# Ten slots for small statistics in place of six, and weight halves that start 128 bytes later in every partition

## The chip, the cores and the metric

The kernel runs on one core of a Trainium2 chip. The metric is the time of one execution on the device, in microseconds; the kernel before takes 1837.65 us, the median of 3 runs. A profiled execution of its own gives the rows shown here: it has the start and the length of each instruction on each engine.

## The reference, cut to what matters

The reference is three transformer layers for 256 tokens of width 1024, in float32. The first block has a retention layer and a differential-attention layer, each with a gated feed-forward net (hidden width 2816); its first layer also carries 256 context tokens. The second block is a token mixer with two attentions and a recurrence, and a squared-ReLU net of hidden width 4096. Nearly all arithmetic is products of a 256-row activation with large weight matrices:

```python
ux = modulate(rms_norm(h_x, norm_g[l, 0]), shm, scm)
p = u @ w_in                                                   # 1024 x 8192, 3072, 6728
val, gate = jnp.split(u @ w_up, 2, axis=-1)
return (jax.nn.silu(dwconv3(gate, conv_w, conv_b)) * val) @ w_down
...
def rms_norm(x, g):
    x32 = x.astype(jnp.float32)
    y = x32 * lax.rsqrt(jnp.mean(x32 * x32, axis=-1, keepdims=True) + EPS)
```

## The kernel before, in words

**Weights in halves.** Weights come from memory one MB at a time into a tile `st` (128 partitions of 2048 floats, two slots). `split_w` cuts each `st` into two tiles `hl`, each of 128 partitions of 2 x 1024 floats (8192 bytes in a partition): part 0 is a rounded copy in the type fp32r, written by ScalarE (L120), and part 1 is the rest that the rounding left, written by VectorE (L121). Tag `hl` has five slots. In a few places the halves go to a slot of tag `big` instead ("wide" halves). Activations are split in the same way into an upper and a lower tile, and these lie in `big` slots always (14 slots of 8192 bytes).

**Three products for one.** With both operands split, each product is three matmuls into one PSUM sum: upper by upper, upper by lower, lower by upper. There are two forms.

- Form A (`mm3`, L129 to L131): the stationary operand is 128 columns of a weight half (`hl`), the moving operand is 256 columns of an activation (`big`). The profile writes it `ps<-big,hl 128x256`.
- Form B (`rows_mm3`, L408 to L410): the stationary operand is 128 columns of an activation (`big`), the moving operand is 512 columns of a weight half (`hl`), written `ps<-hl,big 128x512` or `at<-hl,big 128x512`. The retention product uses form B with both operands in `big` (`at<-big,big`), and so do products with wide halves. `form_b` uses it with 256 columns for the first tiles of the last two up-projections (`ps<-hl,big 128x256`, and `ps<-big,big 128x256` where the halves are wide).

Before each matmul its stationary operand is loaded (row `PEld`); that load runs while the matmul before it still streams its moving operand.

**Small statistics.** `tiny` gives tiles of 1 to 8 floats in a partition, of which each slot takes 32 bytes. `rms2` (L147, L150) and `retain` (L773, L775) write a sum of squares into one, a sum with the epsilon into the next, and `power` (L140, on GpSimd) its inverse square root into a third; `shift_bias` and `top_keys` take some as well. A tag hands its slots out in turn; an instruction that writes a slot waits for what still uses it.

**Where the tags lie.** The pool `sp` lays its tags one behind another in each partition, in the order in which they are first asked for. As the program is built (bytes in a partition, read from its list of allocations):

| tag | slots x bytes | first byte before | first byte after |
|---|---|---|---|
| `mid` | 4 x 4096 | 20,416 | 20,416 |
| `big` | 14 x 8192 | 36,800 | 36,800 |
| `tiny` | 6 (10) x 32 | 151,488 | 151,488 |
| `junk` | 1 x 2048 | 151,680 | 151,808 |
| `sml` | 4 x 2048 | 153,728 | 153,856 |
| `st` | 2 x 8192 | 161,920 | 162,048 |
| `hl` | 5 x 8192 | 178,304 | 178,432 |
| `s1`, `ph_b`, `ph_a` | 5 x 1024, 2 x 2048 | 219,264 | 219,392 |

All operands of both forms start at a multiple of 512 bytes behind the start of their slot. So each start in `big` is 448 beyond a multiple of 512, each start in `hl` 128 beyond one before the change and 256 after it. The text calls "distance" the start of the moving operand less that of the stationary one, counted modulo 512:

| operands | distance before | after |
|---|---|---|
| form A: moving `big`, stationary `hl` | 320 | 192 |
| form B and `form_b`: moving `hl`, stationary `big` | 192 | 320 |
| both in `big` | 0 | 0 |

Of the kernel before, what the change touches and what calls it, by code (L numbers as in the profile page):

```python
# [32 lines left out]
def block_kernel(ctx: ExitStack, tc: tile.TileContext, A, out):  # L33
# [4 lines left out]
    sp = ctx.enter_context(tc.tile_pool(name="sp", bufs=2))  # L38
# [5 lines left out]
    def nm(base):  # L44
        n_name[0] += 1
        return f"{base}_{n_name[0]}"
# [13 lines left out]
        return sp.tile(shape, dt, tag="sml", bufs=4, name=nm("sml"))  # L60

    def tiny(shape, dt=F32):
        return sp.tile(shape, dt, tag="tiny", bufs=6, name=nm("tiny"))

    def junk():
        return sp.tile([P, 512], F32, tag="junk", bufs=1, name=nm("junk"))
# [71 lines left out]
    def power(v, width=1):  # L138
        r = tiny([P, width])
        G.tensor_tensor(r, v, nhalf[:, 0:width], op=ALU.pow)  # L140
        return r

    def rms2(halves, n):

        ss = tiny([P, 2])
        for i in range(2):
            S.activation(junk()[:, 0:halves[i].shape[-1]], halves[i], AF.Square, scale=n ** -0.5,  # L147
                         accum_out=ss[:, i:i + 1])
        v = tiny([P, 1])
        V.tensor_scalar(v, ss[:, 0:1], ss[:, 1:2], EPS, op0=ALU.add, op1=ALU.add)  # L150
        return power(v)
# [1435 lines left out]
```

## Time and profile before

| | |
|---|---|
| median of 3 runs | 1837.65 us (1836.05 to 1839.79) |
| the profiled execution | 1835.11 us |
| its span, first to last instruction | 1833.3 us |
| TensorE busy with matmuls | 1804.6 us, 98% |
| VectorE, ScalarE, GpSimd busy | 1242.5, 897.2, 176.4 us |
| granted TensorE clock | 1.000 |
| DMA queue 1, share of the 16 engines | 52.0% |

The length of a matmul in the profile runs to the end of its results, and it overlaps the next one. What a matmul costs is the distance from its start to the start of the next. The text calls that its pace. A view of a window gives it: of a window in which TensorE never stops, the window and the length of one matmul together (it also counts the ones cut by its edges), divided by the count behind the x. From a timeline it is the start of the last row less that of the first, divided by the rows between.

### The profile page before, as it was taken

What the parts mean: (1) busy time and instruction counts of PE and PEld (TensorE: products, weight loads), DVE (VectorE), ACT (ScalarE), POOL (GpSimd) and SP (SyncE); (2) the same over time, 40 slices, a digit from 0 to 9 for tenths busy, and PEclk for the clock granted to TensorE, in tenths of its full rate; (3) what the DMA queues carried; (4) which work ended last, traced back from release to release, by engine and by line L of the source; (5) the groups of instructions that cost most, each with busy time, mean ns of one, the idle gap of its engine ahead of it and who ended that gap; (6) DMA issues with size and microseconds to landing.
All of it is one profiled execution on the core that took longest, in us unless ns stands there. A gap on an engine that the chain in (4) does not pass through costs nothing.

```text
span 1833.3 us, 28048 instructions
## 1 busy us (share of the span) xinstructions
PE 1804.6 (98%) x11300; PEld 1566.1 (85%) x11300; DVE 1242.5 (68%) x1921; ACT 897.2 (49%) x1460; POOL 176.4 (10%) x178
## 2 busy tenths in 40 slices
PE   9999999999999999999999989999999999999998
PEld 8878787797778999899988766799879999989986
DVE  5874674957567977487847676877664787566644
ACT  6542342323355644364536555754454575455633
POOL 0212212032100000000000020100010001120000
PEclk9999999999999999999999999999999999999999
DMA  8553543738668555555554422455646524545553
GB/s 317 180 193 132 194 151 106 238 127 267 211 235 291 202 185 188 188 174 187 192 201 151 176 93 93 133 176 179 215 155 231 180 93 161 170 161 189 190 188 115
DMA packets 59849, 330.34 MB, mean 180 GB/s; under 512 B 7207, under 2 KB 10424, under 8 KB 27720
## 3 DMA queue, kind: packets, MB, share of 16 engines
q1 hardware_dynamic: 59432, 328.47, 52.0%
q8 instruction: 88, 1.44, 0.3%
q14 instruction: 41, 0.34, 0.1%
q10 hardware_dynamic: 288, 0.09, 0.0%
HBM read 323.75 MB, written 4.79 MB: 179 GB/s over the span
## 4 chain that ended last, share of the span: by engine, by line
PE 85%; DVE 5%; DMA 3%; issue 2%; ACT 2%; POOL 1%; SPq 0%; POOLq 0%; ACTq 0%; DVEq 0%
PE ps L129 10%; PE ps L130 10%; PE ps L131 10%; PE at L408 7%; PE at L410 7%; PE at L409 7%; PE ps L408 6%; PE ps L409 6%; PE ps L410 6%; PE nr L130 2%; PE nr L131 2%; PE nr L129 2%; DVE hl L121 1%; PE at L129 1%; PE at L131 1%
## 5 line engine op out<-in xcount | busy, mean ns | idle before, releaser
L121 DVE TENSOR_TENSOR hl<-st,hl 128x1024 fp32r<-128x1024 f32 x460 | 564.0, 1232 | 343.7 <-ACT hl L120 341.6
L120 ACT ACTIVATE hl<-st 128x1024 fp32r<-128x1024 f32 x462 | 484.9, 1056 | 382.4 <-PE at L410 140.2
L129 PE MATMUL ps<-big,hl 128*128 128x256 f32 x1540 | 433.6, 282 | 1.2 <-DVE s L1324 1.0
L131 PE MATMUL ps<-big,hl 128*128 128x256 f32 x1540 | 430.7, 280 | 0.0
L130 PE MATMUL ps<-big,hl 128*128 128x256 f32 x1540 | 430.5, 280 | 0.0
L129 PEld LDWEIGHTS ps<-big,hl 128*128 128x128 f32 x1540 | 289.4, 188 | 5.7 <-issue 2.3
L130 PEld LDWEIGHTS ps<-big,hl 128*128 128x128 f32 x1540 | 289.6, 188 | 0.4 <-issue 0.2
L131 PEld LDWEIGHTS ps<-big,hl 128*128 128x128 f32 x1540 | 289.2, 188 | 0.1
L408 PE MATMUL ps<-hl,big 128*128 128x512 f32 (+1 forms) x588 | 230.9, 393 | 0.5 <-ACT big L962 0.3
L410 PE MATMUL ps<-hl,big 128*128 128x512 f32 (+1 forms) x588 | 227.5, 387 | 0.9 <-DVE big L316 0.9
L409 PE MATMUL ps<-hl,big 128*128 128x512 f32 (+1 forms) x588 | 227.4, 387 | 0.0
L410 PE MATMUL at<-hl,big 128*128 128x512 f32 x532 | 211.1, 397 | 0.0
L408 PE MATMUL at<-hl,big 128*128 128x512 f32 x532 | 210.7, 398 | 0.2 <-DVE sml L332 0.2
L409 PE MATMUL at<-hl,big 128*128 128x512 f32 x532 | 210.9, 397 | 0.0
L198 DVE SCALAR_TENSOR_TENSOR big<-mid,cs,big 128x1024 f32<-128x1024 f32 x112 | 143.7, 1325 | 11.1 <-DMA mid<-in_ada_w_dram 10.8
L408 PEld LDWEIGHTS ps<-hl,big 128*128 128x128 f32 x588 | 110.7, 188 | 36.5 <-issue 8.1
L410 PEld LDWEIGHTS ps<-hl,big 128*128 128x128 f32 x588 | 110.7, 188 | 25.3 <-DVE big L316 1.3
L409 PEld LDWEIGHTS ps<-hl,big 128*128 128x128 f32 x588 | 110.8, 188 | 23.8 <-DVE hl L121 0.8
L410 PEld LDWEIGHTS at<-hl,big 128*128 128x128 f32 x532 | 100.1, 188 | 24.2 <-issue 0.8
L408 PEld LDWEIGHTS at<-hl,big 128*128 128x128 f32 x532 | 100.0, 188 | 24.2 <-DVE sml L332 0.7
L140 POOL TENSOR_TENSOR tiny<-tiny,nhalf 128x1 f32<-128x1 f32 (+1 forms) x48 | 35.6, 742 | 876.7 <-DVE tiny L150 698.5
L409 PEld LDWEIGHTS at<-hl,big 128*128 128x128 f32 x532 | 100.1, 188 | 23.0
(298 smaller groups left out, 2581.4 us busy)
## 6 DMA issues: line engine op xcount, KB each, us to landing
st<-in_ffn_up_dram SPq DMA_DIRECT2D x66, 1024.0 KB
mid<-in_ada_w_dram SPq DMA_DIRECT2D x80, 512.0 KB
st<-in_ffn_down_dram SPq DMA_DIRECT2D x33, 1024.0 KB
st<-in_mix_in_dram SPq DMA_DIRECT2D x31, 1024.0 KB
st<-in_ret_in_dram SPq DMA_DIRECT2D x28, 1024.0 KB
st<-in_diff_in_dram SPq DMA_DIRECT2D x20, 1024.0 KB
st<-in_ret_out_dram SPq DMA_DIRECT2D x16, 1024.0 KB
st<-in_mlp_up_dram SPq DMA_DIRECT2D x16, 1024.0 KB
```

Of the source, the lines that this page charges most:

```text
L120: S.activation(hl[:, 0, :], src, AF.Copy)
L121: (G if wide // 2 else V).tensor_tensor(hl[:, 1, :], src, f32(hl[:, 0, :]), op=ALU.subtract)
L129: T.matmul(o, lh, rh, start=start, stop=False)
L130: T.matmul(o, lh, rl, start=False, stop=False)
L131: T.matmul(o, ll, rh, start=False, stop=stop)
L140: G.tensor_tensor(r, v, nhalf[:, 0:width], op=ALU.pow)
L198: V.scalar_tensor_tensor(acc[:, s, :], t, cs[:, k, s:s + 1], acc[:, s, :], op0=ALU.mult, op1=ALU.add)
L408: T.matmul(o, xh, wh, start=start, stop=False)
L409: T.matmul(o, xh, wl, start=False, stop=False)
L410: T.matmul(o, xl, wh, start=False, stop=stop)
```

## The change

Tag `tiny` gets ten slots in place of six. Four slots of 32 bytes are 128 bytes, and the tags behind `tiny` lie that much further on. `big` and `mid` stay where they were.

```diff
     def tiny(shape, dt=F32):
-        return sp.tile(shape, dt, tag="tiny", bufs=6, name=nm("tiny"))
+        return sp.tile(shape, dt, tag="tiny", bufs=10, name=nm("tiny"))
```

No instruction is added, taken away or moved on any engine. What differs in the order are waits. On ScalarE, in the four retention products of the second head (`retain`), the piece of the difference reads as follows (each L773 writes the sums of one product, each L120 is an upper weight half of the next product):

```order
 L773 ACTIVATE junk_1326,tiny_1312<-at_1314 128x512 [waits PE_49,Activation_49]
-L773 ACTIVATE junk_1348,tiny_1336<-at_1337 128x512 [waits DVE_49,PE_49,Activation_49]
+L773 ACTIVATE junk_1348,tiny_1336<-at_1337 128x512 [waits PE_49,Activation_49]
 L773 ACTIVATE junk_1362,tiny_1336<-ps_1338 128x512 [waits PE_49,Activation_49]
-L773 ACTIVATE junk_1387,tiny_1372<-at_1373 128x512 [waits DVE_49,PE_49,Activation_49]
+L773 ACTIVATE junk_1387,tiny_1372<-at_1373 128x512 [waits PE_49,Activation_49]
 L773 ACTIVATE junk_1398,tiny_1372<-at_1374 128x512 [waits PE_49,Activation_49]
 L693 ACTIVATE big_1408<-ps_1417 128x256 [waits PE_49,Pool_49]
-L120 ACTIVATE hl_1659<-st_1654 128x1024 [waits PE_49]
+L120 ACTIVATE hl_1659<-st_1654 128x1024 [waits DVE_49,PE_49]
```

The wait of the sums for VectorE, which read the slot two products earlier, goes; the weight halves behind it now name VectorE themselves.

## Rows read from the trace of the kernel before

**Rows 1.** The page: busy time, DMA queue, and the chain that ended last
```profile
PE 1804.6 (98%) x11300; PEld 1566.1 (85%) x11300; DVE 1242.5 (68%) x1921; ACT 897.2 (49%) x1460; POOL 176.4 (10%) x178
...
q1 hardware_dynamic: 59432, 328.47, 52.0%
...
PE 85%; DVE 5%; DMA 3%; issue 2%; ACT 2%; POOL 1%; SPq 0%; POOLq 0%; ACTq 0%; DVEq 0%
PE ps L129 10%; PE ps L130 10%; PE ps L131 10%; PE at L408 7%; PE at L410 7%; PE at L409 7%; PE ps L408 6%; PE ps L409 6%; PE ps L410 6%; PE nr L130 2%; PE nr L131 2%; PE nr L129 2%; DVE hl L121 1%; PE at L129 1%; PE at L131 1%
```

**Rows 2.** Groups by line and shape: xcount | busy us, mean ns | idle before
```profile
L121 DVE TENSOR_TENSOR hl<-st,hl 128x1024 fp32r<-128x1024 f32 x460 | 564.0, 1232 | 343.7 <-ACT hl L120 341.6
L129 PE MATMUL ps<-big,hl 128*128 128x256 f32 x1540 | 433.6, 282 | 1.2 <-DVE s L1324 1.0 <-ACT s L1107 0.2
...
L408 PE MATMUL ps<-hl,big 128*128 128x512 f32 x540 | 217.3, 402 | 0.3 <-ACT big L962 0.3
...
L408 PE MATMUL at<-hl,big 128*128 128x512 f32 x532 | 210.7, 398 | 0.2 <-DVE sml L332 0.2
...
L129 PE MATMUL nr<-big,hl 128*128 128x256 f32 x240 | 67.1, 280 | 0.0
L129 PE MATMUL at<-big,hl 128*128 128x256 f32 x220 | 62.7, 285 | 1.5 <-DVE s L1324 1.5
...
L408 PE MATMUL at<-big,big 128*128 128x512 f32 x108 | 42.7, 400 | 0.6 <-DVE big L778 0.6
...
L408 PE MATMUL ps<-hl,big 128*128 128x256 f32 x48 | 13.6, 283 | 0.2
```

**Rows 3.** Windows of form A (distance 320), TensorE alone: busy (count), clock, DMA
```profile
core 0: us, PE busy (x), PEclk, DMA share, GB/s
620.00:720.00 100.00, 100.00 (x851) 1.00 0.55 186
...
1212.00:1300.00 88.00, 88.00 (x750) 1.00 0.55 186
1681.00:1736.00 55.00, 55.00 (x469) 1.00 0.57 189
```

**Rows 4.** The same view: the first, the longest and the last of seven other windows
```profile
1192.00:1198.00 6.00, 6.00 (x55) 1.00 0.47 188
1402.00:1427.00 25.00, 25.00 (x223) 1.00 0.62 216
...
1662.00:1667.50 5.50, 5.50 (x51) 1.00 0.34 140
```

**Rows 5.** Timeline of two runs with 256 columns moving from `hl`, first and last
```profile
1184.65 0.28 PE L408 MATMUL ps<-hl,big 128*128 128x256 f32 x1
...
1186.89 0.28 PE L409 MATMUL ps<-hl,big 128*128 128x256 f32 x1
...
1653.03 0.28 PE L410 MATMUL ps<-hl,big 128*128 128x256 f32 x1
...
1656.09 0.28 PE L410 MATMUL ps<-hl,big 128*128 128x256 f32 x1
```

**Rows 6.** Timeline of a run with 256 columns, both operands in `big`, first and last
```profile
1187.48 0.28 PE L408 MATMUL ps<-big,big 128*128 128x256 f32 x1
...
1190.96 0.28 PE L410 MATMUL ps<-big,big 128*128 128x256 f32 x1
```

**Rows 7.** 512 columns: a window from `hl`; first and last of a run from `big`
```profile
1740.00:1820.00 80.00, 80.00 (x345) 1.00 0.49 168
...
250.48 0.39 PE L408 MATMUL at<-big,big 128*128 128x512 f32 x1
...
261.81 0.39 PE L410 MATMUL at<-big,big 128*128 128x512 f32 x1
```

**Rows 8.** What ended the idle time before line L773: us, times
```profile
  PE at L410: 8.5, 7
  issue: 7.3, 4
```

## The prediction

> **What bounds the kernel now.** I read the page first. TensorE is busy for 98% of the span and stands for 85% of the chain that ended last; VectorE, the next, is busy for 68% [rows 1]. In the groups by line, almost no idle time stands before the matmuls of form A and form B: 1.2 us before 1540 of them, 0.3 us before 540 [rows 2]. So the time is a sum of paces of matmuls. The granted clock is 1.00 (the 2.4 GHz level) in all windows used below [rows 3, 4, 7], so no difference of pace among them comes from the clock.
>
> Then I read paces from windows in which TensorE never stops. Form A runs at (100 + 0.28) / 851 = 117.8 ns, and again at 117.7 and 117.9 ns in windows far apart [rows 3]. But in seven other windows, with 491 counted matmuls, the same form with operands in the same tags runs at 113.4 ns (25.28 / 223) or close to it [rows 4]. So form A has a narrow and a wide pace, 4.4 ns apart. A long window of either holds it to its end: what a stretch begins with, it keeps. The address alone does not decide it, since nothing differs between those windows in the starts modulo 512.
>
> The place of the operands does matter. With 256 columns and both operands in `big` (distance 0) the pace is 3.48 us over 29 steps, 120.0 ns [rows 6]. With the moving operand in `hl` (distance 192) one run has 3.06 us over 27 steps, 113.3 ns, and another 2.24 us over 19 steps, 117.9 ns [rows 5]: the two paces of form A again. With 512 columns from `hl` the pace is 80.39 / 345 = 233.0 ns, and with both in `big` 11.33 us over 50 steps, 226.6 ns [rows 7]. Shape, type and clock are the same in each pair, and only the tag of an operand differs. The next stationary operand is loaded while the moving one streams, both out of the same partitions; a likely reading is that the two reads get in each other's way more or less by where they lie. That reading is mine; the paces are the trace's.
>
> **The change part by part.** It changes two things.
>
> First, waits. The statistics in `tiny` no longer wait for a slot's reader of two products ago. What ended ScalarE's idle time before L773 is the matmul whose result it squares, or "issue", 7.3 us in 4 places; no reader of a slot stands there [rows 8]. The order of all engines is the same. I take 0, with bounds of 0 and 7.3 us gained, if all of that "issue" were the slot and all lay on the path. A loss is excluded: a wait taken out cannot come later, and the waits that now name VectorE before L120 ask for work that the old wait ahead of it on ScalarE had already covered.
>
> Second, addresses. `st` moves by 128 bytes too, as a target of DMA; the queue's packets take 52.0% of the engines' time [rows 1], so twice nothing is lost there even if each packet took some per cent longer or shorter: 0. ScalarE and VectorE read and write `st` and `hl`; an L121 takes 1232 ns and stands 343.7 us idle in all [rows 2], so some per cent either way there is hidden under the matmuls: 0.
>
> What is left is the matmuls. Form A has three times 1540 + 240 + 220, that is 6000 of them; form B from `hl` has three times 540 + 532, that is 3216 [rows 2]. The change swaps their distances: form A goes from 320 to 192, form B from 192 to 320. Products with both operands in `big` keep theirs.
>
> *Form A.* The only rows that show 256 columns at distance 192 are those of `form_b` (48 a line [rows 2]). Both paces occur there. I count its stretches in the timeline as mostly narrow; the wide one of [rows 5] follows a pause. In form A now, the seven narrow windows hold 491 of 6000, so about 5500 are wide. Bounds: all narrow, 5500 x 4.4 = 24 us gained; all at the pace of distance 0, 5500 x 2.2 + 500 x 6.6 = 15 us lost. I take four fifths of the 5500 narrow: 5500 x 0.8 x 4.4 = 19.4 us gained, because distance 192 is the nearest row. Form A's lines have about 38% of the chain [rows 1], 697 us, against 6000 x 117.4 = 704 us of pace: nearly all of it counts.
>
> *Form B.* No row shows 512 columns at distance 320. The nearest are 226.6 ns at distance 0 and 233.0 ns at 192. Bounds: the step of 6.4 ns down, 3216 x 6.4 = 21 us gained, and the same step up, 21 us lost. There is no reason in the rows for either, and the pace from `hl` is one value in the long stretches; I take 0.
>
> The sum: 1835.1 us of the profiled execution, less 19.4, is 1815.7. The median of the runs shown is 2.5 us above that execution, so I expect 1818 us.
>
> A rule of the Trainium skill speaks against any effect. "TensorE: Matmul & The Clock Gate", part 2, says that TensorE has two independent read ports into SBUF, and that loading the next weights takes no bandwidth from the matmul that runs; it gives a pace of N / 2.4 + 2.5 ns, 109 ns for 256 columns and 216 ns for 512. By that rule the change is worth 0. The trace does not agree: 113.4, 117.8 and 120.0 ns for one shape, 226.6 and 233.0 ns for the other [rows 3 to 7].
>
> **The rivals.**
>
> *Nothing changes.* The distances 320 and 192 differ by 128 and both leave 64 modulo 128, while distance 0 leaves 0. If only that remainder counts, all paces stay. For it: the two paces of form A and of `form_b` are equal, 117.8 and 113.4 against 117.9 and 113.3 ns [rows 3 to 5]. Against it: how seldom form A is narrow now. It gives 1837.7 us, and less the bound of the waits 1830. The skill's rule of two ports ends here too.
>
> *Form B slows by a step.* Slower: 3216 x 6.4 = 21 us, if form A stays as it is; 1858 us. The place is each product with weights moving, above all the last stretch, 80 us at 233.0 ns without a pause [rows 7]. It decides as soon as the pace of form B rises more than 6 ns, for then 19.4 us of form A no longer pay for it. For it: between distance 0 and 192 the two shapes went opposite ways (120.0 to 113.3 ns with 256 columns, 226.6 to 233.0 with 512), so a swap that helps the one may hurt the other. Against: by that same pattern form B would go down if form A's old 117.8 ns is what distance 320 means.
>
> *Both gain.* Form B falls to the 226.6 ns of distance 0 and form A becomes narrow: 1818 less 21, 1797 us.
>
> **How the numbers follow.** A measurement of this kernel tells about 0.2%, 3.7 us, from no change. Chances: one of the two forms gains about 20 us, 0.36 (mostly form A, my forecast); both gain, 0.08; the waits alone gain more than 3.7 us, 0.01. Faster: 0.45. Nothing changes, or form A's gain is eaten by form B: 0.27. Form B slower with form A as it is, 0.16, form A slower toward 120.0 ns, 0.09, both slower, 0.03: slower, 0.28. The range, 1796 to 1858 us, reaches from both gaining to form B's step up and leaves out some 1 in 10. Where only form A's share of narrow stretches is uncertain, from a third of the 24 us gained to all of it, the range of the forecast itself is 1813 to 1830 us.
>
> **What would show it.** In the profile after, the windows of long form A stretches, now near 117.8 ns, should stand at 113.4 ns, and the last stretch of form B at 233 ns still. The mean length of L129 should fall below 282 ns. TensorE's idle time, the lengths of L120 and L121 and the DMA share should not move. I am wrong if the pace of form A stays at 117.8 ns, or if form B's last stretch leaves 233 ns by more than 2 ns; which of the two moved, and by how much, then gives the time: 6 us for each nanosecond of form A, 3.2 us for each of form B.

## The result, and the profile after

The changed kernel takes 1806.08 us, the median of 4 runs (1804.03 to 1808.72); beside it, the kernel before takes 1836.85 us (also 4 runs). The ratio is 0.9836, with a 95% interval of 0.9824 to 0.9849; the medians lie 30.8 us apart. The forecast was 1818 us in a range of 1796 to 1858, faster with a chance of 0.45. The profiled execution takes 1804.03 us, with a span of 1802.2 us, 31.1 us below that of before, at a mean granted clock of 0.999.

The page of the changed kernel, with the lines that answer to [rows 1]:

```profile
PE 1776.8 (99%) x11300; PEld 1547.9 (86%) x11300; DVE 1242.6 (69%) x1921; ACT 896.4 (50%) x1460; POOL 173.3 (10%) x178
...
q1 hardware_dynamic: 59432, 328.47, 52.7%
...
PE 88%; DVE 5%; issue 2%; ACT 2%; DMA 1%; POOL 1%; SPq 0%; POOLq 0%; DVEq 0%; ACTq 0%
```

TensorE's busy time fell by 27.8 us with the same 11300 matmuls, its idle time from 28.7 to 25.4 us. VectorE, ScalarE and the packets of the queue did what they did before: 52.7% of 1802.2 us is 950 us, 52.0% of 1833.3 us was 953. So nearly all of the time came out of the matmuls themselves. The groups by line and shape, as in [rows 2]:

```profile
L121 DVE TENSOR_TENSOR hl<-st,hl 128x1024 fp32r<-128x1024 f32 x460 | 565.9, 1237 | 316.8 <-ACT hl L120 314.1
...
L129 PE MATMUL ps<-big,hl 128*128 128x256 f32 x1540 | 430.2, 279 | 0.8 <-DVE s L1324 0.7
...
L408 PE MATMUL ps<-hl,big 128*128 128x512 f32 x540 | 216.6, 401 | 0.3 <-ACT big L962 0.3
...
L408 PE MATMUL at<-hl,big 128*128 128x512 f32 x532 | 207.6, 392 | 0.3 <-DVE sml L332 0.3
```

L129 fell from 282 to 279 ns, and L408 with `at` from 398 to 392. These are lengths that overlap; what a matmul costs is its pace, and the windows give that. Windows of TensorE alone, the first three in form A and the last in form B (they answer to [rows 3] and [rows 7]; the same stretches come some 8 to 31 us earlier now):

```profile
core 0: us, PE busy (x), PEclk, DMA share, GB/s
612.00:708.00 96.00, 96.00 (x849) 1.00 0.55 190
...
1192.00:1276.00 84.00, 84.00 (x743) 1.00 0.56 191
1655.00:1706.00 51.00, 51.00 (x452) 1.00 0.56 195
...
1709.00:1794.00 85.00, 85.00 (x373) 1.00 0.48 161
```

Form A: 96.28 / 849 = 113.4 ns, and again 84.28 / 743 = 113.4 and 51.28 / 452 = 113.5, where 117.8 stood. Form B: 85.39 / 373 = 228.9 ns, where 233.0 stood. Both forms became faster at the same clock. Not all of form A did. The next windows of the same kernel show two pairs, each a stretch of form A with a stretch of form B right behind it:

```profile
148.00:169.00 21.00, 21.00 (x180) 1.00 0.25 87
171.00:186.00 15.00, 15.00 (x66) 1.00 0.46 142
711.00:769.00 58.00, 58.00 (x255) 1.00 0.59 203
```

In the first of them form A, at 148 us, is wide, 21.28 / 180 = 118.2 ns, and form B behind it has 15.39 / 66 = 233.2 ns. The form A stretch at 612 us is narrow, and form B behind it, at 711 us, has 58.39 / 255 = 229.0. The experiments come back to this.

Since the trace has the start of each matmul, all steps from one start to the next can be added up by form:

| steps, added up, in us | before | after | |
|---|---|---|---|
| form A, 6000 | 715.6 | 695.5 | -20.1 |
| form B from `hl`, 3215 | 761.2 | 750.8 | -10.4 |
| the other products of both forms | 160.1 | 160.3 | +0.2 |
| all other matmuls | 187.4 | 186.7 | -0.7 |

The sum is -31.0 us, and the span fell by 31.1. Such steps also hold TensorE's waits; those that follow one another without a break, taken alone, fell by 17.9 us in form A and by some 12 in form B from `hl`, so the paces stand for nearly all of it. Of the steps of form A that follow one another without a break, 12% were narrow (up to 115 ns) before and 80% after. A "break" here and below is a wait, or some matmuls of another kind, such as the transposes of L290, which part two stretches.

### The profile page after: what moved, and what is told of

Its sections match the earlier page's. It is cut to its first block, busy times and chain, and to the rows that moved or that the text cites. A ratio compares the mean times of both kernels' runs of the same rounds, so it can differ in the third digit from the quotient of the medians.

```text
span 1802.2 us, 28063 instructions
## 1 busy us (share of the span) xinstructions
PE 1776.8 (99%) x11300; PEld 1547.9 (86%) x11300; DVE 1242.6 (69%) x1921; ACT 896.4 (50%) x1460; POOL 173.3 (10%) x178
## 3 DMA queue, kind: packets, MB, share of 16 engines
q1 hardware_dynamic: 59432, 328.47, 52.7%
## 4 chain that ended last, share of the span: by engine, by line
PE 88%; DVE 5%; issue 2%; ACT 2%; DMA 1%; POOL 1%; SPq 0%; POOLq 0%; DVEq 0%; ACTq 0%
PE ps L129 10%; PE ps L130 10%; PE ps L131 10%; PE at L410 7%; PE at L408 7%; PE at L409 7%; PE ps L408 7%; PE ps L410 7%; PE ps L409 6%; PE nr L131 2%; PE nr L130 2%; PE nr L129 2%; PE at L129 1%; PE at L131 1%; PE at L130 1%
## 5 line engine op out<-in xcount | busy, mean ns | idle before, releaser
L121 DVE TENSOR_TENSOR hl<-st,hl 128x1024 fp32r<-128x1024 f32 x460 | 565.9, 1237 | 316.8 <-ACT hl L120 314.1
L120 ACT ACTIVATE hl<-st 128x1024 fp32r<-128x1024 f32 x462 | 484.0, 1056 | 348.8 <-PE at L410 100.5
L129 PE MATMUL ps<-big,hl 128*128 128x256 f32 x1540 | 430.2, 279 | 0.8 <-DVE s L1324 0.7
L129 PEld LDWEIGHTS ps<-big,hl 128*128 128x128 f32 x1540 | 289.3, 188 | 5.3 <-issue 2.3
L408 PE MATMUL ps<-hl,big 128*128 128x512 f32 (+1 forms) x588 | 230.2, 392 | 0.5 <-ACT big L962 0.3
L410 PE MATMUL ps<-hl,big 128*128 128x512 f32 (+1 forms) x588 | 226.5, 385 | 0.8 <-DVE big L316 0.8
L410 PE MATMUL at<-hl,big 128*128 128x512 f32 x532 | 210.1, 395 | 0.0
L408 PE MATMUL at<-hl,big 128*128 128x512 f32 x532 | 207.6, 392 | 0.3 <-DVE sml L332 0.3
L408 PEld LDWEIGHTS ps<-hl,big 128*128 128x128 f32 x588 | 110.8, 188 | 35.1 <-issue 6.8
L410 PEld LDWEIGHTS ps<-hl,big 128*128 128x128 f32 x588 | 110.8, 188 | 24.1 <-DVE big L316 1.2
L408 PEld LDWEIGHTS at<-hl,big 128*128 128x128 f32 x532 | 99.9, 188 | 22.6 <-DVE sml L332 0.7
L410 PEld LDWEIGHTS at<-hl,big 128*128 128x128 f32 x532 | 100.0, 188 | 20.8 <-issue 0.8
```

What stands on the lines that cost most here:

```text
L120: S.activation(hl[:, 0, :], src, AF.Copy)
L121: (G if wide // 2 else V).tensor_tensor(hl[:, 1, :], src, f32(hl[:, 0, :]), op=ALU.subtract)
L129: T.matmul(o, lh, rh, start=start, stop=False)
L408: T.matmul(o, xh, wh, start=start, stop=False)
L410: T.matmul(o, xl, wh, start=False, stop=stop)
```

## The experiments

**The theories.** *Distance:* the pace of a matmul depends on how far apart its two operands start in a partition. *Waits:* the four further slots let the statistics go ahead, and the matmuls only look faster. *Place:* what counts is where `hl`, `st` or another tag lies by itself, not in relation to `big`. Below, the remainder is the distance modulo 256; why 256 is one of the results. All kernels are variants of the kernel before, so the comparison is with that. It was run again beside each group of them, with medians from 1834.80 to 1835.98 us, and each ratio is to its own group's.

**1. The bytes without the slots** (`pad128`). Six slots, and an unused tile of 128 bytes behind `tiny`.

```diff
-        return sp.tile(shape, dt, tag="tiny", bufs=6, name=nm("tiny"))
+        t = sp.tile(shape, dt, tag="tiny", bufs=6, name=nm("tiny"))
+        if not padded:
+            padded.append(sp.tile([P, 32], F32, tag="pad", bufs=1, name="pad"))
+        return t
```

> Six slots of tiny as before, and an unused tile of 128 bytes behind them, so that hl starts at 178,432 as after the change. Theory D (the distance of the moving from the stationary start, modulo 512, sets the pace): 1806 us within 4, form A near 113.4 ns in the long stretches, form B 228.9 ns. Theory H (hl's own place, modulo 256, sets it): the same. Theory W (the ten slots, by the waits that they take away): 1837 us, form A 117.8 ns, form B 233.3 ns.

Measured: 1808.52 us, ratio 0.9848 [0.9834, 0.9863]. Its windows in form A and form B:

```profile
612.00:708.00 96.00, 96.00 (x850) 1.00 0.55 190
1714.00:1798.00 84.00, 84.00 (x368) 1.00 0.47 162
```

96.28 / 850 = 113.3 ns and 84.39 / 368 = 229.3 ns: the paces of the changed kernel, and an interval that overlaps that of the changed kernel. The bytes alone give the gain.

**2. The slots without the shift** (`slots22`). 22 slots move `hl` by 16 x 32 = 512 bytes.

```diff
-        return sp.tile(shape, dt, tag="tiny", bufs=6, name=nm("tiny"))
+        return sp.tile(shape, dt, tag="tiny", bufs=22, name=nm("tiny"))
```

> Twenty-two slots of tiny and nothing else: hl starts 512 bytes later than before, at the same place modulo 512. Theories D and H: no change from before, 1837 us within 4, form A 117.8 ns, form B 233.3 ns, and so 512 bytes is a multiple of the period. Theory W: 1806 us, as after the change, since even more waits are gone. If the paces change to yet other values, the period is longer than 512 bytes.

Measured: 1835.54 us, ratio 0.9998 [0.9988, 1.0007]. A form A window, 617 to 717 us:

```profile
617.00:717.00 100.00, 100.00 (x852) 1.00 0.55 187
```

100.28 / 852 = 117.7 ns, as before. More slots, without a new distance, are worth nothing, to within some 2 us. *Waits* has fallen.

**3. Everything moved by 128 bytes** (`both128`). An unused tile of 128 bytes ahead of `big`, so that `big` and all tags behind it move together.

```diff
+        if not pad_b:
+            pad_b.append(sp.tile([P, 32], F32, tag="pad_b", bufs=1, name="pad_b"))
```

> Six slots of tiny, and an unused tile of 128 bytes ahead of big: big and hl both lie 128 bytes later. hl is where the change put it, the distances are those of before (320 and 192). Theory D: 1837 us within 4, form A 117.8 ns, form B 233.3 ns. Theory H: 1806 us, 113.4 and 228.9 ns.

Measured: 1835.22 us, ratio 1.0001 [0.9991, 1.001].

```profile
618.00:718.00 100.00, 100.00 (x851) 1.00 0.56 189
```

117.8 ns. `hl` and `st` lie where the changed kernel has them, modulo 512, and nothing is gained.

**4. The distance, with `hl` at its old place** (`big384`). 384 bytes ahead of `big` and 128 behind `tiny`: `hl` and `st` lie 512 bytes further on, and the distances are those of the changed kernel.

```diff
+            pad_b.append(sp.tile([P, 96], F32, tag="pad_b", bufs=1, name="pad_b"))
...
+            padded.append(sp.tile([P, 32], F32, tag="pad", bufs=1, name="pad"))
```

> Six slots of tiny, an unused tile of 384 bytes ahead of big and one of 128 bytes behind tiny: hl lies 512 bytes later than before, at its old place modulo 512, big 384 bytes later. The distances are those of after the change (192 and 320). Theory D: 1806 us within 4, form A 113.4 ns in the long stretches, form B 228.9 ns. Theory H: 1837 us, 117.8 and 233.3 ns.

Measured: 1815.41 us, ratio 0.989 [0.9874, 0.9907]. Three stretches of form A, each with the form B stretch right behind it:

```profile
611.00:711.00 100.00, 100.00 (x851) 1.00 0.56 190
713.00:772.00 59.00, 59.00 (x255) 1.00 0.57 196
1201.00:1286.00 85.00, 85.00 (x752) 1.00 0.55 191
1288.00:1341.00 53.00, 53.00 (x233) 1.00 0.62 209
1665.00:1718.00 53.00, 53.00 (x470) 1.00 0.57 194
1720.00:1805.00 85.00, 85.00 (x373) 1.00 0.47 161
```

Two thirds of the gain come back, so with runs 1 and 3 *place* as the cause by itself has fallen and *distance* stands. Why only two thirds, the rows tell: the first form A stretch is wide here, 100.28 / 851 = 117.8 ns, and form B behind it has 59.39 / 255 = 232.9 ns. The other two are narrow, 113.4 ns both, and form B behind them has 229.1 and 228.9. Of form A's unbroken steps 51% are narrow, and its steps add up to 7.5 us more than in the changed kernel. The four runs lie between 1814.45 and 1817.21 us, all above the slowest of the changed kernel, so this is not an accident of the one profiled execution. At one distance form A has both paces, and form B, where it follows form A without a break, is wide behind a wide stretch and narrow behind a narrow one.

**5. Four other distances** (`pad64`, `pad192`, `pad256`, `pad320`). As run 1, with 64, 192, 256 and 320 bytes in place of 128, that is 16, 48, 64 and 80 floats; the first of them:

```diff
-            padded.append(sp.tile([P, 32], F32, tag="pad", bufs=1, name="pad"))
+            padded.append(sp.tile([P, 16], F32, tag="pad", bufs=1, name="pad"))
```

> An unused tile of 64 bytes behind six slots of tiny: hl 64 bytes later than before, distance of form A 256, of form B 256. Theory D gives no row for it. If the pace runs straight from distance 192 to 320 it lies between: form A 115 to 118 ns, form B 231 ns, about 1822 us. If only the remainder modulo 128 counted beside the step found (0 against 64), both forms would stand as with both operands in big: 120 and 227 ns, 1830 us.

> The same with 192 bytes: form A at distance 128, form B at 384. If the pace runs on in the direction from before to after: form A at 113.4 ns in more stretches, form B near 225 ns, about 1785 us. If the remainder modulo 128 counts, as pad64: about 1830 us.

> The same with 256 bytes: form A at distance 64, form B at 448. If the period is 256 bytes, the paces are those of before: 117.8 and 233.3 ns, 1837 us. If it is 512, they are others, and by the direction seen so far form A is wide or narrow as its stretches begin and form B is below 228.9 ns: about 1790 us.

> The same with 320 bytes: hl stands at the same place modulo 512 as big, so every product of both forms has distance 0. Theory D: form A at the 120.0 ns and form B at the 226.6 to 227.4 ns that products with both operands in big have: 6000 x 2.6 slower and 3200 x 6.3 faster than before, about 1832 us. A theory in which the tag counts and not the distance has no reason for just these two values.

Measured: `pad64` 1833.11 us, 0.9992 [0.9982, 1.0002]; `pad192` 1841.2 us, 1.0037 [1.0024, 1.0051]; `pad256` 1834.93 us, 1.0003 [0.9991, 1.0015]; `pad320` 1833.3 us, 0.9994 [0.9984, 1.0003]. A window of form A and one of form B from `pad64`:

```profile
614.00:714.00 100.00, 100.00 (x836) 1.00 0.53 181
1740.00:1820.00 80.00, 80.00 (x354) 1.00 0.49 168
```

from `pad192`:

```profile
618.00:718.00 100.00, 100.00 (x845) 1.00 0.54 183
1745.00:1825.00 80.00, 80.00 (x346) 1.00 0.50 171
```

from `pad256`:

```profile
619.00:719.00 100.00, 100.00 (x851) 1.00 0.55 189
1740.00:1820.00 80.00, 80.00 (x345) 1.00 0.48 166
```

and from `pad320`:

```profile
612.00:712.00 100.00, 100.00 (x836) 1.00 0.53 182
1740.00:1820.00 80.00, 80.00 (x355) 1.00 0.50 171
```

`pad320` puts both forms at distance 0, and they have the paces that both operands in `big` have [rows 6, 7]: 100.28 / 836 = 120.0 ns, and 80.39 / 355 = 226.5 ns. So it is the distance and not the tag. `pad64` (256 for both forms) counts 836 and 354 in the same lengths, and `pad256` counts 851 and 345 as the kernel before does. So the pace repeats with a period of 256 bytes. `pad192`, remainder 128, has 118.7 and 232.3 ns; it is slower than before. That the two kernels at remainder 0, `pad64` and `pad320`, end close to the time of before is two large terms against each other: form A's steps grow from 715.6 to 732.0 us in `pad64`, and form B's fall from 761.2 to 742.6.

**6. 32 bytes to either side** (`pad96`, `pad160`). As run 1 with 96 and 160 bytes, 24 and 40 floats; the first of them:

```diff
-            padded.append(sp.tile([P, 32], F32, tag="pad", bufs=1, name="pad"))
+            padded.append(sp.tile([P, 24], F32, tag="pad", bufs=1, name="pad"))
```

> The unused tile behind tiny has 96 bytes: by the period of 256 bytes that the runs so far show, form A is at distance 224 and form B at 32, between the place of pad64 (0 and 0; 120 and 227.3 ns) and that of after (192 and 64; 113.4 or 117.8, and 228.9 ns). If the pace changes by whole steps of 64 bytes of distance, it equals one of these two: 1833 or 1806 us. If it runs between them, about 1818 us. If 32 bytes out of step helps both, it is below 1806 us.

> The unused tile has 160 bytes: form A at distance 160, form B at 96, between the place of after (192 and 64) and that of pad192 (128 and 128; 118.9 and 232.6 ns). By whole steps of 64 bytes: 1806 or 1841 us. Running between them: about 1823 us. If 32 bytes out of step helps both, it is below 1806 us.

Measured: `pad96` 1839.47 us, 1.0023 [1.0013, 1.0032]; `pad160` 1838.07 us, 1.0012 [1.0003, 1.0021]. Form A and form B in `pad96`:

```profile
618.00:718.00 100.00, 100.00 (x848) 1.00 0.54 186
1742.00:1822.00 80.00, 80.00 (x345) 1.00 0.49 169
```

and in `pad160`, with a second window of form A:

```profile
620.00:720.00 100.00, 100.00 (x845) 1.00 0.55 188
1743.00:1823.00 80.00, 80.00 (x345) 1.00 0.49 168
1212.00:1300.00 88.00, 88.00 (x752) 1.00 0.57 192
```

Form A has 118.3 ns in the one, and 118.7 and 117.4 in the other; form B 233.0 in both. 32 bytes off, the whole gain is gone.

**7. Form B's distance alone** (`b_alone`). Each half gets a slot of 2096 floats and starts in it at one of four places 64 bytes apart, chosen by its slot and by the form that will read it. Form A and `form_b` keep the remainders of before (64 and 192), and form B gets 64. The first row of places is for halves that form A or `form_b` will read, the second for those of form B, and the calls of `wchunks` and `split_w` say which. 96 bytes of constants were packed to make room.

```diff
+    START = ((0, 16, 32, 48, 0), (32, 48, 0, 16, 32))
+    def half_tile(rows):
+        n = n_hl[0]
+        o = START[rows][(0, 4, 3, 2, 1)[n] if n < 5 else (3, 0, 2, 4, 1)[n % 5]]
+        n_hl[0] += 1
+        t = sp.tile([P, 2096], F32R, tag="hl", bufs=5, name=nm("hl"))
+        return t[:, o:o + 2048].rearrange("p (a c) -> p a c", a=2)
```

> Six slots as before. Each weight half gets a slot 192 bytes longer than itself and a start inside it that depends on the form that will read it, so that form A and form_b keep the distances of the kernel before (64 and 192, modulo 256) and form B alone gets that of the changed kernel (64 modulo 256). Theory (each form has its pace by its own distance): form A as before, 117.5 ns, form B from 233.3 down to about 229 ns, so 3216 x 3.8 = 12 us gained: about 1824 us. Rival 1 (form B gained because the form A stretches beside it had become narrow): no gain, 1836 us. Rival 2 (only the common place of all halves counts, whatever the form): 1836 us or 1806 us.

Measured: 1829.18 us, ratio 0.9968 [0.9956, 0.9979]: half of what was expected. Three stretches of form A, each with form B right behind it, and ahead of them a stretch of form B that follows a break:

```profile
200.00:231.00 31.00, 31.00 (x137) 1.00 0.53 181
613.00:713.00 100.00, 100.00 (x851) 1.00 0.55 187
715.00:774.00 59.00, 59.00 (x254) 1.00 0.57 196
1203.00:1289.00 86.00, 86.00 (x761) 1.00 0.56 192
1290.00:1344.00 54.00, 54.00 (x238) 1.00 0.62 212
1671.00:1726.00 55.00, 55.00 (x470) 1.00 0.55 187
1728.00:1815.00 87.00, 87.00 (x374) 1.00 0.46 157
```

Behind wide form A (117.8 ns) form B runs at 59.39 / 254 = 233.8 ns, behind narrow form A (113.4 ns) at 54.39 / 238 = 228.5. Both the theory and its rival were half right: remainder 64 lets form B run at 229 ns, but a stretch that follows wide form A without a break does not get it. The last pair is wide again, 117.6 and 87.39 / 374 = 233.7 ns. Behind a break form B needs no form A: the first window has 31.39 / 137 = 229.1 ns, and in the four kernels with remainder 64 for form B (the changed one and runs 1, 4 and 7) every stretch of form B of 20 or more matmuls behind a break runs at 228.9 to 230.0 ns by the starts in the trace, all 15 right behind narrow form A at 228.9, and all 17 right behind wide form A at 233.3 or 233.4. In the profiled execution, at 1825.55 us the second fastest of ten, form B's steps add up to 754.6 us, 6.5 less than before, in place of the 12 expected; form A's, with 19% narrow, are 3.8 less.

**8. The best distance for each form** (`two_starts`). The same, with remainder 192 for form A and 0 for form B; `form_b` at 64.

```diff
-    START = ((0, 16, 32, 48, 0), (32, 48, 0, 16, 32))
+    START = ((32, 48, 0, 16, 32), (16, 32, 48, 0, 16))
```

> The same slots and starts by form, with the best distance seen for each: form A 192 modulo 256 as in the changed kernel, form B 0 modulo 256, the distance at which both kernels run their products with both operands in big (227 ns). form_b keeps 64. Theory: form A gains 20 us as in the changed kernel, form B 3216 x 6.0 = 19 us, together about 1797 us, 9 us below the changed kernel; the rest that TensorE waits for may grow and leave 1801 us. Rival (the forms are not independent, and the gain of form A comes only with form B at 64): 1817 us or more.

Measured: 1807.98 us, ratio 0.9852 [0.984, 0.9865]: faster than before, and not faster than the changed kernel. Two pairs again, and a stretch of form A between them:

```profile
608.00:708.00 100.00, 100.00 (x851) 1.00 0.55 189
710.00:768.00 58.00, 58.00 (x257) 1.00 0.58 200
1194.00:1279.00 85.00, 85.00 (x753) 1.00 0.56 190
1658.00:1711.00 53.00, 53.00 (x470) 1.00 0.58 197
1713.00:1797.00 84.00, 84.00 (x372) 1.00 0.48 163
```

Form B did its part: 58.39 / 257 = 227.2 and 84.39 / 372 = 226.9 ns, whatever ran ahead of it, and its steps add up to 744.0 us, 6.8 less than in the changed kernel. Form A did not: the long stretches at 608 and 793 us are wide here, 117.8 ns, the ones at 1194 and 1658 us narrow. Of its unbroken steps 41% are narrow, where the changed kernel has 80%, and its steps add up to 706.2 us, 10.7 more. Whether the new distance of form B made the difference is not told by this run: run 4, with both distances of the changed kernel, has 51%.

## Why the prediction was right, and where it was off

**What bounds the kernel** held. The time is a sum of paces: the unbroken steps of the two forms fell by some 30 of the 31.1 us, and TensorE's idle time, which should not have moved, fell by 3.3.

**Waits, taken at 0,** held. Run 2 is the measure. What became of the 7.3 us of "issue" ahead of L773 [rows 8] the changed kernel shows in the same view:

```profile
  PE at L410: 16.7, 13
  PE ps L410: 6.3, 5
```

The "issue" row is gone, and the wait for the product of L410 whose result L773 squares grew from 8.5 us to 16.7, by more than the 7.3 us that went. ScalarE waits for TensorE there, with more slots or fewer.

**Addresses of `st`, L120 and L121, taken at 0,** held. L121 went from 1232 to 1237 ns and is hidden. Runs 3 and 4 took `st` along with `hl`: at its new place modulo 512 without a gain, and at its old one with it.

**Form A, taken at -19.4 us,** held, in mechanism and in size: -20.1. The step that carried it, that distance 192 is that of `form_b`, whose stretches were mostly narrow, was read from 144 matmuls. Four fifths of the wide ones was a choice; it leaves 4900 of 6000, 82%, narrow, and 80% came out. Run 4, with the same distances and 51%, shows that this share could have been another: that the size came out as well is in part luck. The mirror held as well: `form_b`, now at 320, is wide. First and last matmul of a run of 36 in the changed kernel, to set against [rows 5]:

```profile
1625.51 0.28 PE L408 MATMUL ps<-hl,big 128*128 128x256 f32 x1
...
1629.63 0.28 PE L410 MATMUL ps<-hl,big 128*128 128x256 f32 x1
```

4.12 us over 35 steps is 117.7 ns.

**Form B, taken at 0,** is the term that was mis-sized: -10.4 us, most of the 12 us by which the forecast was too high. The time lies in the range, but the mechanism was right for one form of two. "There is no reason in the rows for either" was the step. The forecast's own condition for being wrong, a last stretch that leaves 233 ns by more than 2, was met: 228.9. One row did give a reason, and stood under the rival of form B's step: by the pattern that the two shapes went opposite ways, form B would go down where form A's old pace was what distance 320 meant. That is what happened, with a smaller step than the 6.4 ns that were the bound. The bound itself, the pace of distance 0, is right only for distance 0.

**The rivals.** *Nothing changes* has fallen: remainders 64 and 192 modulo 256 differ, and 128 is not the period. With it falls, for this kernel, a single pace for each shape: one shape shows 113.4 to 120.0 ns, the other 226.5 to 233.8, by the place of the operands. "TensorE: Matmul & The Clock Gate", part 2, of the Trainium skill gives one pace, 109 ns for the one shape and 216 ns for the other; the trace does not agree. The same part of the Trainium skill says that loading weights takes no read bandwidth from the matmul that runs; no run here tests that by itself. *Form B slows* has fallen too. *Both gain*, to which the prediction gave a chance of 0.08, is what happened: the right signs and the right parts. Its 1797 us took 21 us for form B where there were 10.

**What stays open.** That the distance sets which paces are possible is shown by runs 1 to 6. Why is only argued: the load of a stationary operand runs beside the streaming of a moving one (the loads are busy for 86% of the span of the changed kernel, the matmuls for 99%), and their reads may meet or miss each other by where they lie. Within a form the matmul's own stationary operand and the next one lie at the same distance, and no run told them apart. What decides, behind a break, whether a stretch of form A becomes narrow or wide is open as well. The distance bears on how often: at remainder 64 the narrow share of form A's unbroken steps was 5 to 19% in five kernels (that of before, runs 2, 3 and 7, and `pad256`), at remainder 192 it was 41, 51, 79 and 80% in four (runs 8, 4 and 1, and the changed kernel). What makes 41 or 80 of it is not known; run 4 has the distances of the changed kernel at other places, so that the places bear on this share is not excluded. Why form B at remainder 64 follows form A's pace is not known either.

## What to carry to other kernels

Where TensorE never stops, read the pace of each form window by window and by the tags of its operands; where one shape shows several paces at one clock, the start addresses are a parameter like a tile size. An unused tile of some bytes tells it in one run, and it should be run through a whole period in small steps, since here one of the five shifts within the period that were run (64, 96, 128, 160 and 192 bytes) gave the gain, and those 32 bytes to either side of it none. Don't add up the best pace of each form: measure them together, since a stretch may take its pace over from the one ahead of it.

## What the runs showed of the hardware that was not expected

The paces by the remainder of the distance modulo 256, from the windows above, those of before and, for 128, the starts of the matmuls in the trace, all at a granted clock of 1.00 (the 2.4 GHz level):

| remainder, bytes | form A, ns | form B, ns |
|---|---|---|
| 0 | 120.0 | 226.5 to 227.2 |
| 32 | not run | 233.0 |
| 64 | 117.8, seldom 113.4 | some 229 (228.5 to 229.3) or some 233 (232.9 to 233.8) |
| 96 | not run | 233.0 |
| 128 | 118.7, or 120.0 in stretches of 192 and 239 matmuls | 232.3 |
| 160 | 117.4 or 118.7 | not run |
| 192 | 113.4 or 117.8 | 233.0 |
| 224 | 118.3 | not run |

- The period is 256 bytes: 256 and 512 bytes more (`pad256`, run 2) give the paces and the time of before, and distance 256 the paces of distance 0.
- The two forms want different distances. Remainder 0 is the best for 512 columns and the worst for 256.
- At remainder 64 form B has two paces, and where a form A stretch runs right ahead of it, it follows that one: 229 ns behind 113.4, 233 behind 117.8, in the changed kernel and in runs 1, 4 and 7. Behind a break it has 229. At remainder 0 it has one pace, whatever ran ahead.
- No stretch of form A of 100 or more matmuls changed its pace on the way, in any of the 14 kernels: the longest, of 863 matmuls, have the same pace in each third, to within 0.1 ns.
